# Eight PSUM banks dealt anew: four for the scores, one in two halves for the attention's outputs

## The chip, the cores and the metric

The kernel runs on one core of one Trainium2 chip. The metric is the device time of one execution in microseconds (us); before the change it is 2353.01 us, the median of three runs (2352.11 to 2354.78).

## What is computed

One inference step of a transformer layer with two kinds of attention side by side. For 2048 new frames of one stream and for 16 new frames of each of 8 running streams (with 512 cached frames each):

```
h  = rms_norm(x) * (1 + scale) + shift          # modulation from c @ w_ada
qa, ka, va, za, qb, kb, vb, zb, ga, gb = split(h @ w_in)
oa = (softmax(q1 k1) - lam * softmax(q2 k2)) @ va    # 4 heads, width 2 x 64, rotated q and k
ob = a @ vb                                          # 8 heads, width 64, where, with z = q.k / 8:
     a[q,k] = sigmoid(z[q,k]) * product over j > k of sigmoid(-z[q,j])      # "stick breaking"
ya = (rms_norm(oa) * silu(za)) @ w_branch_a;  yb = (ob * silu(zb)) @ w_branch_b
x  = x + gate * ((sigmoid(ga) * ya + sigmoid(gb) * yb) @ w_out)
y  = rms_norm(x)
```

Both masks are causal (by chunks of 64 for the first kind). The outputs are y and the new keys and values.

## The kernel before

Matrix operands are held as pairs of 16-bit numbers, a high and a low part, so a product takes up to three matmuls. Work goes by tiles of 128 rows: 16 tiles of the new stream, and tile number 16 (NT) for the 8 x 16 running frames.

**First stage** (some 145 us). `modulation` multiplies the conditioning by w_ada; `modulated` (L1052) scales and turns x by matmuls with a diagonal (L1065) into h, which is stored in HBM as hT_d.

**Attention.** Eight units follow one another: unit u is head u // 2 of the softmax kind (kind 0, even u) or a pair of stick-breaking heads (kind 1, odd u). Each unit goes through 17 tiles. For each tile `project` multiplies h by the unit's weights: 24 matmuls into a bank "mm" (L427), and in six of the eight units as much again for a gate, into bank "t" (L494). ACT, DVE and POOL turn the result into q, k and v. `transpose_qk` turns q and k through bank "t" (L507, L511; evacuated in L521, L522). `scores` makes the scores of one tile against all keys up to it, in chunks of up to 512 keys: two matmuls into a bank "s" (L629, L630), and a mask on the diagonal chunk (L633). A softmax chunk is read by DVE with a running maximum (L548). A stick-breaking chunk is read by ACT, which puts sigmoid(z) into SBUF and sigmoid(-z) back into the bank (both by the helper at L119), and then by a DVE scan along the keys (L606), which makes the products; POOL multiplies (L612). `turn` splits the weights into high and low parts (L562, L563, or L290, L295) and has SP's queue turn them by a transposing DMA into one of five tiles wt (L570). Two steps later `pv` multiplies them by v: three matmuls per block of 128 keys for kind 0 (L677 to L679), two for kind 1 (L681, L682), for both heads of the pair. The sum of one tile grows in a bank "o"; such a run of matmuls into one output is called a group. `natural` reads it out: ACT for kind 0 (L658), ACT and then DVE for kind 1 (L663, L664). There are 8 x 16 = 128 groups.

**Last stage** (from about 1805 us). For each tile, `inputs` and `transposed` (L1141, through bank "s") prepare the merged attention outputs, `branches` multiplies by the branch weights (L1289, bank "mm"), `output` by w_out in two halves of 512 columns (L1318, each half in a bank "o"). Beside it runs `sample`, the attention of the running streams over their caches (L745 to L753, banks "s"; L784, bank "t").

PSUM has eight banks of 128 x 512 numbers of 32 bits, and `BANKS` (L185) deals them out: 2 "mm", 3 "s", 1 "t", 2 "o". A tile of a tag takes the next free bank of that tag; where none is free, its first matmul waits for the readers of an earlier tile. In the first stage L1063 takes banks "s" and "o" in turn.

**What sets the order.** The program lists the pieces of a step (projection, scores, outputs) interleaved by estimated costs (`interleave`, L91; outputs between 0.1 and 1.0 of the step, V_LO and V_HI). From that list a scheduler makes the order of the instructions of each engine when the program is built: it goes through its own estimate of the time, and gives each engine the earliest listed instruction that is ready by it, a free bank included. On the chip each engine then runs its instructions in that fixed order, and waits by semaphores where the data or the bank isn't ready. All loads, stores and transposes are issued in order by SP: the h tiles (L404, three buffers hs), the transposes (L570), the stores of k, v and z (L475, L476, L478) and of outputs (L671).

Of the kernel before, what the change touches and what calls it, by code (L numbers as in the profile page):

```python
# [16 lines left out]
F32 = mybir.dt.float32  # L17
# [8 lines left out]
P = 128  # L26
# [83 lines left out]
def layer_kernel(ctx: ExitStack, tc: tile.TileContext, a: dict):  # L110
# [40 lines left out]
    def x_rows(t):  # L151
        return x_p[t * P : (t + 1) * P, :] if t < NT else x_s
# [17 lines left out]
    ps = ctx.enter_context(tc.tile_pool(name="ps", bufs=2, space=bass.MemoryType.PSUM))  # L170
# [11 lines left out]
    kvp = c01.enter_context(tc.tile_pool(name="kvp", bufs=2))  # L182
    stg = c01.enter_context(tc.tile_pool(name="stg", bufs=2))

    BANKS = {"mm": 2, "s": 3, "t": 1, "o": 2}  # L185

    def bank(tag, dt=F32):
        return ps.tile([P, 512 if dt == F32 else 1024], dt, tag=tag, name=f"ps_{tag}", bufs=BANKS[tag])

# [462 lines left out]
    def natural(U, t, po, pool=stg):  # L652

        kind = U["kind"]
        o = pool.tile([P, P], F32, tag="o", name="o")
        s = U["sc"][:, 5:6]
        if kind == 0:
            S.activation(out=o, in_=po[:, 0:P], func=AF.Identity, scale=s)  # L658
            return o
        ob = pool.tile([P, P], F32, tag="ob", name="ob", bufs=1)  # L660
        p4 = po[:, 0 : 2 * P].rearrange("p (c f d) -> p c f d", c=2, f=2)
        oh, ol = (x.rearrange("p (c d) -> p c d", c=2) for x in (ob, o))
        S.activation(out=oh, in_=p4[:, :, 1, :], func=AF.Identity, scale=s)  # L663
        V.scalar_tensor_tensor(out=ol, in0=p4[:, :, 0, :], scalar=s, in1=oh, op0=ALU.mult, op1=ALU.add)  # L664
        return o

    def store(U, t, o):
        ui = (U["h"] + 4 * U["kind"]) * P
        if U["kind"] == 0:
            sum_squares(o, P, osums[:, t, U["h"] : U["h"] + 1])  # L670
        load(out=o_d[t][:, ui : ui + P], in_=o)  # L671

    def pv_block(job, seg, po, wj, vt, first, last):

        wt, nb, c = seg["wt"], seg["hi"] - seg["lo"], job["c"]
        if job["U"]["kind"] == 0:
            T.matmul(po[:, 0:P], wt[:, wj, :], vt[:, :, 0, :], start=first, stop=False)  # L677
            T.matmul(po[:, 0:P], wt[:, wj, :], vt[:, :, 1, :], start=False, stop=False)
            T.matmul(po[:, 0:P], wt[:, nb + wj, :], vt[:, :, 0, :], start=False, stop=last)  # L679
        else:  # L680
            T.matmul(po[:, c * P : (c + 1) * P], wt[:, wj, :], vt[:, c, :, :], start=first, stop=False)  # L681
            T.matmul(po[:, c * P : c * P + 64], wt[:, nb + wj, :], vt[:, c, 0, :], start=False, stop=last)  # L682

    def pv(job):

        U, t, c = job["U"], job["t"], job["c"]
        segs = job["segs"] if U["kind"] == 0 else job["segs"][::-1]
        order = [(seg, j) for seg in segs for j in range(seg["hi"] - seg["lo"])]

        def block(i):  # L690
            seg, j = order[i]
            if i == 0 and (U["kind"] == 0 or c == 0):
                U["po", t] = bank("o")
            pv_block(job, seg, U["po", t], j, U["v"][seg["lo"] + j], i == 0, i == len(order) - 1)
            if i == len(order) - 1 and (U["kind"] == 0 or c == 1):
                store(U, t, natural(U, t, U.pop(("po", t))))

        return [(1.5, lambda i=i: block(i)) for i in range(len(order))]
# [194 lines left out]
    with tc.tile_pool(name="p0", bufs=1) as p0:  # L893
# [8 lines left out]
        def hp_tile(dt):  # L902
            hp = p0.tile([P, 4096], F32, tag="hp", name="hp", bufs=3)
            return hp.bitcast(dt) if dt != F32 else hp
# [23 lines left out]
        pt = bank("t")  # L928
# [33 lines left out]
        pt = bank("t")  # L962
# [89 lines left out]
        def modulated(g):  # L1052

            t0, w = GROUPS[g]
            nt = w // P
            box = {}

            def piece(k):
                if k == 0:
                    box["hp"] = hp = hp_tile(F16)[:, 0 : nt * 2 * D].rearrange("p (i a k n) -> p i a k n", a=2, k=KT, n=P)  # L1060
                    at_hand.update({t0 // P + i: hp[:, i, :, :, :] for i in range(nt)})
                hp = box["hp"]
                pt = bank("so"[k % 2])  # L1063
                for i in range(nt):
                    T.matmul(pt[:, i * P : (i + 1) * P], xs[g][i][:, k * P : (k + 1) * P], diags[g][:, i, :], start=True, stop=True)  # L1065
                tmp = p0.tile([P, 512], F32, tag="tmp", name="tmp", bufs=2)
                hi, lo = hp[:, :, 0, k, :], hp[:, :, 1, k, :]
                pv = pt[:, 0:w].rearrange("p (i n) -> p i n", n=P)
                tv = tmp[:, 0:w].rearrange("p (i n) -> p i n", n=P)
                if t0 < SEQ:  # L1070
                    S.activation(out=hi, in_=pv, func=AF.Identity, scale=ab[:, 0, k, 0:1], bias=ab[:, 1, k, 0:1])
                    V.tensor_scalar(out=tv, in0=pv, scalar1=ab[:, 0, k, 0:1], scalar2=ab[:, 1, k, 0:1],
                                    op0=ALU.mult, op1=ALU.add)
                else:
                    tb = tmp[:, 0:w].rearrange("p (b s) -> p b s", b=NB)
                    V.tensor_tensor(out=tb, in0=pt[:, 0:w].rearrange("p (b s) -> p b s", b=NB),
                                    in1=ab[:, 0, k, 1:9].unsqueeze(2).to_broadcast([P, NB, NS]), op=ALU.mult)
                    V.tensor_tensor(out=tb, in0=tb, in1=ab[:, 1, k, 1:9].unsqueeze(2).to_broadcast([P, NB, NS]), op=ALU.add)
                    S.copy(out=hi, in_=tv)
                G.tensor_tensor(out=lo, in0=tv, in1=hi, op=ALU.subtract)  # L1080
                if k == KT - 1:
                    load(out=hT_d[g], in_=hp)

            return [(1.0, lambda k=k: piece(k)) for k in range(KT)]

        def gates():
# [136 lines left out]
    for n in range(len(steps) + PV_LAG):  # L1223
        made, qk, vs = [], [], []
        if n < len(steps):
            u, t = steps[n]
# [28 lines left out]
    with ExitStack() as c2:  # L1255
# [16 lines left out]
        def gate_rows(i, n):  # L1272

            pg = bank("t")
            gsm = s2.tile([P, 512], F32, tag="sg", name="gsm", bufs=2)
            load(out=gsm[0:9, :], in_=gate_d[:, n * 512 : (n + 1) * 512])
            T.matmul(pg, sel[0:9, i * P : (i + 1) * P], gsm[0:9, :], start=True, stop=True)
            return pg
# [27 lines left out]
        def output(t, st, box):  # L1306

            def half(j):
                if j == 0:
                    box["x"] = s2.tile([P, D], F32, tag="x", name="x2", bufs=2)  # L1310
                    load(out=box["x"], in_=x_rows(t))
                x = box["x"]
                c = slice(j * 512, (j + 1) * 512)
                po = bank("o")
                n = 0
                for yi, wi in ((0, 0), (0, 1), (1, 0)):
                    for k in range(KT):
                        T.matmul(po, st["y"][:, yi * 8 + k, :], wo[j * 4 + k // 2][:, wi, k % 2, :], start=(n == 0), stop=(n == 3 * KT - 1))  # L1318
                        n += 1
                m = s2.tile([P, 512], F32, tag="sg", name="m", bufs=2)  # L1320
                if t < NT:
                    V.scalar_tensor_tensor(out=m, in0=po, scalar=st["f"][:, 1:2], in1=gate[:, c], op0=ALU.mult, op1=ALU.mult)
                else:
                    S.activation(out=m, in_=po, func=AF.Identity, scale=st["f"][:, 1:2])
                    V.tensor_tensor(out=m, in0=m, in1=gate_rows(1, j), op=ALU.mult)
                G.tensor_tensor(out=x[:, c], in0=m, in1=x[:, c], op=ALU.add)
            return [(5.2, lambda j=j: half(j)) for j in range(2)]
# [73 lines left out]
```

## Time and profile before

| | |
|---|---|
| median of three runs | 2353.01 us |
| the profiled execution | 2352.26 us |
| its span, first to last instruction | 2350.5 us |
| PE (matmul) busy | 2124.5 us, 90% |
| DVE (vector) busy | 1729.8 us, 74% |
| ACT (scalar) busy | 1635.9 us, 70% |
| POOL busy | 687.0 us, 29% |
| DMA | 453.74 MB, mean 193 GB/s |
| TensorE clock granted, mean | 0.965 of full speed |

Lines named Lnnn are lines of the kernel before. PE is the matmul engine, PEld its weight loads, SP the queue that issues DMAs. A row of waits reads "who waits, the tile and line it waits to write <- whom it waits for: us in total, times, longest us". A row of groups reads "line, engine, operation, out<-in, shapes, count | busy us, mean ns of one | idle us of the engine before it <- what ended that idle time". A row of the timeline reads "start us, length us, engine, line, operation, tiles, shapes, count". Matmuls overlap in the records: one of 512 columns is shown with 380 ns, but a new one starts about every 0.22 us.

### The profile page before, as it was taken

The numbers are of one execution on the slowest core, as the hardware profiler recorded it, in microseconds if no ns is written. First come the engines' busy times: TensorE is split into PE (matmuls) and PEld (weight loads), VectorE is DVE, ScalarE is ACT, GpSimd is POOL, SyncE is SP. The second block draws the span as 40 slices with busy tenths as digits, with TensorE's granted clock in tenths as the row PEclk, the third lists the DMA queues.
The fourth block names the chain that finished last, engine by engine and source line by source line (L and its number), as shares of the span: only waits on it lengthen the run. The fifth ranks groups of instructions, "written<-read, shape, count | busy, mean of one in ns | idle before, by whom it ended". The sixth has DMA issues, their size and how long they took to land. (4 is left out here: it accounts for less than half of the span.)

```text
span 2350.5 us, 42534 instructions
## 1 busy us (share of the span) xinstructions
PE 2124.5 (90%) x15272; PEld 1147.0 (49%) x15272; DVE 1729.8 (74%) x3604; ACT 1635.9 (70%) x3148; POOL 687.0 (29%) x563
## 2 busy tenths in 40 slices
PE   5898898998999899899999989999995789889998
PEld 3554454444555444445554544555553344445453
DVE  4847865779775567988666798867678777878763
ACT  4557777777786777778677787866677666666541
POOL 1533012345310233632023364203334222222221
PEclk8999999999999999999999999999997899999999
DMA  9766669887795898878678796866677999998621
GB/s 336 254 203 175 158 137 252 196 195 158 188 238 134 192 222 195 174 171 197 137 178 204 170 196 171 203 150 162 151 170 166 290 254 255 282 238 239 178 100 55
DMA packets 843572, 453.74 MB, mean 193 GB/s; under 512 B 538234, under 2 KB 786346, under 8 KB 842848
## 3 DMA queue, kind: packets, MB, share of 16 engines
q1 hardware_dynamic: 842412, 450.63, 77.2%
q8 instruction: 119, 1.95, 0.3%
q14 instruction: 93, 0.76, 0.1%
q10 hardware_dynamic: 948, 0.39, 0.1%
HBM read 249.80 MB, written 73.44 MB: 138 GB/s over the span
## 5 line engine op out<-in xcount | busy, mean ns | idle before, releaser
L612 POOL TENSOR_TENSOR sc_p<-sc_p,sc_n 128x127 f32<-128x127 f32 (+7 forms) x192 | 311.3, 1625 | 885.5 <-DVE sc_n L606 870.5
L427 PE MATMUL ps_mm<-wb,hs 128*128 128x512 f16 x1632 | 413.4, 380 | 5.0 <-DMA hs<-hT_d 3.2
L427 PEld LDWEIGHTS <-hs 128*128 128x128 f16 x3120 | 273.8, 99 | 252.3 <-issue 12.5
L427 PE MATMUL ps_mm<-wa,hs 128*128 128x512 f16 x1488 | 378.4, 385 | 3.4 <-DVE v L295 2.4
L606 DVE TENSOR_TENSOR_SCAN sc_n<-ps_s,sc_n,zero_t 128x512 f32<-128x512 f32 x192 | 245.3, 1278 | 75.6 <-ACT ps_s L119 72.5
L629 PE MATMUL ps_s<-k,qst 128*128 128x512 f16 (+3 forms) x640 | 225.7, 354 | 47.2 <-DVE sc_n L606 33.7
L563 DVE TENSOR_TENSOR sc_n<-sc_p,sc_n 128x128 f16<-128x128 f32 (+7 forms) x192 | 219.9, 1150 | 51.3 <-ACT sc_n L562 50.8
L494 PEld LDWEIGHTS <-hs 128*128 128x128 f16 x1632 | 154.8, 98 | 182.9 <-DVE qst L522 7.8
L119 ACT ACTIVATE sc_p<-ps_s,usc 128x512 f32<-128x512 f32 (+3 forms) x320 | 203.7, 636 | 44.9 <-PE ps_s L630 34.7
L630 PE MATMUL ps_s<-k,qst 128*128 128x512 f16 (+3 forms) x640 | 225.6, 354 | 0.0
L681 PE MATMUL ps_o<-v,wt 128*128 128x128 f16 x1088 | 175.3, 226 | 36.3 <-DMA wt<-sc_n 36.2
L562 ACT CAST sc_n<-sc_p 128x128 f16<-128x128 f32 (+7 forms) x192 | 154.5, 808 | 65.7 <-POOL sc_p L612 65.0
L494 PE MATMUL ps_t<-wb,hs 128*128 128x512 f16 x816 | 193.5, 381 | 7.0 <-DVE qst L522 6.9
L119 ACT ACTIVATE ps_s<-ps_s,usc 128x512 f32<-128x512 f32 (+3 forms) x328 | 198.6, 606 | 0.0
L494 PE MATMUL ps_t<-wa,hs 128*128 128x512 f16 x816 | 192.1, 380 | 1.7 <-ACT qst L522 1.7
L1318 PE MATMUL ps_o<-wo,wb 128*128 128x512 f16 x816 | 188.6, 386 | 0.7 <-ACT wb L1142 0.7
L682 PE MATMUL ps_o<-v,wt 128*128 128x64 f16 x1088 | 160.1, 198 | 0.0
L681 PEld LDWEIGHTS <-wt 128*128 128x128 f16 x1088 | 106.3, 102 | 104.6 <-DMA wt<-sc_n 48.2
L606 DVE TENSOR_TENSOR_SCAN sc_n<-ps_s,zero_t 128x128 f32<-128x128 f32 (+3 forms) x128 | 104.3, 815 | 48.4 <-ACT ps_s L119 46.3
L548 DVE TENSOR_SCALAR_CACHE_REDUCE sc_p<-ps_s,usc 128x512 f32<-128x512 f32 (+3 forms) x160 | 106.1, 664 | 42.3 <-PE ps_s L630 27.2
L682 PEld LDWEIGHTS <-wt 128*128 128x128 f16 x1088 | 103.9, 101 | 56.3 <-issue 1.9
L548 DVE TENSOR_SCALAR_CACHE_REDUCE sc_n<-ps_s,usc 128x512 f32<-128x512 f32 (+3 forms) x160 | 106.2, 664 | 31.5 <-PE ps_s L630 13.7
(345 smaller groups left out, 4478.0 us busy)
## 6 DMA issues: line engine op xcount, KB each, us to landing
hs<-hT_d SPq DMA_DIRECT2D x130, 512.0 KB, 4.5
g_d<-gt SPq DMA_DIRECT2D x68, 256.0 KB, 4.2
wb<-g_d SPq DMA_DIRECT2D x26, 512.0 KB, 5.7
out_dram<-pr SPq DMA_DIRECT2D x204, 64.0 KB, 2.1
z_d<-pr SPq DMA_DIRECT2D x136, 64.0 KB, 1.8
o_d<-o SPq DMA_DIRECT2D x136, 64.0 KB, 2.4
hs<-z_d SPq DMA_DIRECT2D x17, 512.0 KB, 5.0
hs<-o_d SPq DMA_DIRECT2D x17, 512.0 KB, 6.4
```

What stands on the lines that cost most here:

```text
L119: i = S.activation(**kw)
L427: T.matmul(box["p"], box["h"][:, hi, k, :], U["w"][k][:, wi, :], start=(n == 0), stop=(n == 3 * KT - 1))
L494: T.matmul(box["g"][:, 0:gw], box["h"][:, hi, k, :], U["wg"][k // per][:, k % per, wi, :], start=(j == 0), stop=(j == 3 * KT - 1))
L548: V.tensor_scalar(out=dst[:, lo : lo + n], in0=p[:, 0:n], scalar1=sc_pos, scalar2=None, op0=ALU.mult, op1=ALU.max, accum_out=job["mx"][:, ...
L563: V.tensor_tensor(out=lo, in0=src, in1=hi, op=ALU.subtract)
L606: V.tensor_tensor_scan(out=dst[:, lo : lo + n][:, ::-1], data0=src[:, 0:n][:, ::-1], data1=zero_t[:, 0:1].to_broadcast([P, n]), initial=fi ...
L612: G.tensor_tensor(out=p[:, 0:m], in0=p[:, 0:m], in1=n[:, 1 : m + 1], op=ALU.mult)
L629: T.matmul(p[:, 0:n], qst[:, c, :], kk[:, c, 0:n], start=True, stop=False)
L630: T.matmul(p[:, 0:n], qst[:, 2 + c, :], kk[:, c, 0:n], start=False, stop=not diag)
L681: T.matmul(po[:, c * P : (c + 1) * P], wt[:, wj, :], vt[:, c, :, :], start=first, stop=False)
L682: T.matmul(po[:, c * P : c * P + 64], wt[:, nb + wj, :], vt[:, c, 0, :], start=False, stop=last)
L1318: T.matmul(po, st["y"][:, yi * 8 + k, :], wo[j * 4 + k // 2][:, wi, k % 2, :], start=(n == 0), stop=(n == 3 * KT - 1))
```

## The change

The banks are dealt anew: four for "s", none for "o", and one tile `outputs_of` that is allocated once and takes the eighth bank. The attention's outputs use its columns 0 to 255 and 256 to 511 in turn, one group after the other. A softmax group uses 128 of its 256 columns, a stick-breaking group all 256. The first stage's turns use "s" alone. In the last stage the first half of an output tile uses the whole of `outputs_of`, the second a bank "s". In what follows, line numbers are those of the kernel before.

```diff
-    BANKS = {"mm": 2, "s": 3, "t": 1, "o": 2}
+    BANKS = {"mm": 2, "s": 4, "t": 1}
+
+    outputs_of = ps.tile([P, 512], F32, tag="o", name="ps_o", bufs=1)
+    out_at = [0]
...
             if i == 0 and (U["kind"] == 0 or c == 0):
-                U["po", t] = bank("o")
+                out_at[0] ^= 1
+                U["po", t] = outputs_of[:, out_at[0] * 256 : out_at[0] * 256 + 256]
...
-                pt = bank("so"[k % 2])
+                pt = bank("s")
...
-                po = bank("o")
+                po = bank("s") if j else outputs_of
```

No instruction is added or removed: matmuls, evacuations and DMAs are the same in number and shape. The scheduler makes its order anew.

## The prediction

> **What bounds the kernel now.** I read the page's span first, then the busy time of each engine by stage (windows cut where the attention's score matmuls begin, near 145 us, and where the attention's last scores have run, near 1805 us), then PE's waits inside the attention, then the chain that ended last.
>
> ```profile
> span 2350.5 us, 42534 instructions
> ```
>
> ```profile
> 0.00:145.00 145.00, 112.51 (x761) 72.58 (x762) 85.68 (x239) 69.72 (x132) 59.03 (x73) 0.91 0.79 266
> 145.00:1805.00 1660.00, 1536.84 (x10773) 830.51 (x10770) 1251.51 (x2545) 1249.27 (x2572) 510.99 (x411) 0.98 0.77 181
> 1805.00:2350.00 545.00, 475.20 (x3740) 243.88 (x3740) 392.63 (x821) 316.93 (x446) 116.98 (x81) 0.94 0.79 210
> ```
>
> The columns after the length are PE, PEld, DVE, ACT and POOL busy time, then PE's granted clock, the DMA share and GB/s. In the attention PE works 1536.8 of 1660 us; DVE and ACT reach 75% each. So PE is the engine to follow, and what can be won without taking matmuls away is its 123 us of idle time. What ended that idle time:
>
> ```profile
> PE ps_s L629 <- DVE sc_n L606: 33.7, 41, 2.3
> PE ps_o L681 <- DMA wt<-sc_n: 25.9, 24, 2.4
> PE ps_o L677 <- DMA wt<-sc_n: 18.4, 13, 3.1
> PE ps_s L629 <- DVE sc_p L548: 9.4, 8, 3.8
> PE ps_t L507 <- DVE k L295: 7.8, 9, 1.7
> PE ps_t L494 <- DVE qst L522: 6.9, 4, 3.3
> PE ps_t L507 <- ACT gt L497: 4.5, 6, 1.1
> PE ps_mm L427 <- DVE v L295: 4.2, 2, 2.4
> PE ps_mm L427 <- DMA hs<-hT_d: 4.0, 4, 1.6
> PE ps_s L629 <- DVE sc_n L548: 3.7, 3, 2.3
> PE ps_t L494 <- ACT qst L522: 1.7, 1, 1.7
> ```
>
> Each row has the sum, the number of times and the longest, in us. The eleven make 120.2, nearly all of the 123. Three kinds matter. **Score banks** (L629 waits for the reader of a bank to let it go): 33.7 + 9.4 + 3.7 = 46.8. **Turned weights** (L681, L677 wait for a transposing DMA): 25.9 + 18.4 = 44.3. **The projection's side** (the other six): 29.1. No row shows PE waiting for an output bank.
>
> PE's queue is in order, so such a stall delays all that is behind it. From 2208 us to 2340 the chain that ended last is nearly all matmuls, as in this piece:
>
> ```profile
> 2295.17 8.85 PE ps_o L1318 x41
> 2304.02 0.89 PE ps_s L1141 x16
> ```
>
> So what PE saves in the attention is not covered by a slower engine at the end.
>
> **The change, part by part.** It adds and removes no matmul, no evacuation and no DMA. It changes which bank is written, and the scheduler, which knows the banks, then gives another order to the same instructions. I compare both orders as built, counting matmuls, and turn counts into time with this row of the timeline:
>
> ```profile
> 481.10 5.34 PE L494 MATMUL ps_t<-wa,hs 128*128 128x512 f16 x24
> ```
>
> 24 matmuls of 512 columns in 5.34 us: 0.22 us each. The narrow matmuls of the outputs take less, so times from counts are upper estimates.
>
> *1. A fourth bank for the scores.* A bank of a stick-breaking chunk is held through two sigmoids and a scan:
>
> ```profile
> L606 DVE TENSOR_TENSOR_SCAN sc_n<-ps_s,sc_n,zero_t 128x512 f32<-128x512 f32 x192 | 245.3, 1278 | 75.6 <-ACT ps_s L119 72.5
> ...
> L119 ACT ACTIVATE sc_p<-ps_s,usc 128x512 f32<-128x512 f32 x224 | 157.2, 702 | 38.7 <-PE ps_s L630 34.7 <-PE ps_s L633 3.8
> ...
> L119 ACT ACTIVATE ps_s<-ps_s,usc 128x512 f32<-128x512 f32 x224 | 151.6, 677 | 0.0
> ```
>
> 0.70 + 0.68 + 1.28 = 2.66 us at least, beyond the matmuls. In the built order, between the last matmul in such a bank and the first of its next tenant stand 50 other matmuls at the median before, 67 after (37 and 48 for the softmax heads); 247 of the score matmuls carry a wait for the scan before, 161 after. 17 more matmuls are about 3.7 us of lead, against a mean wait of 33.7 / 41 = 0.8 us and a longest of 2.3. Bounds: 46.8 gained, or 0, if ACT and DVE fall back as far as the scores run ahead. I take 28, a little over the drop in the count, for lead is long against the waits.
>
> *2. Turned weights.* With scores earlier, a stick-breaking segment has 195 matmuls between its last score and the first use of its turned weights, 162 before. But weights that wait longer hold one of five wt buffers longer, and SP, whose queue is also in order, already stands for them:
>
> ```profile
> SPq L404 <- PE ps_t L494: 61.8, 25, 8.1
> SPq L570 <- PE ps_o L682: 51.6, 30, 4.0
> ```
>
> 145 of the transposes wait for PE to free a buffer in the built order before, 180 after. Behind each waiting transpose stand the stores of keys, values and outputs, the weight loads and the next h tile (L404). Bounds: 44.3 gained; or a loss of 51.6 x 35 / 145 = 12.5, if SP's extra standing came through to PE whole. I take a gain of 10.
>
> *3. One bank for the outputs.* Halves in turn look like two buffers. Who reads an output:
>
> ```profile
> L658 ACT ACTIVATE o<-ps_o,usc x64: 345/365/382, 163.7 to 1601.1; 128x128 f32<-128x128 f32 x64
> L663 ACT ACTIVATE ob<-ps_o,usc x64: 343/372/459, 341.0 to 1820.4; 128x128 f32<-128x128 f32 x64
> L664 DVE SCALAR_TENSOR_TENSOR o<-ps_o,usc,ob x64: 319/330/351, 342.0 to 1820.8; 128x128 f32<-128x128 f32 x64
> ```
>
> As built, the first output matmul of a group waits for the readers of the group just before it in 104 of 128 groups (16 before): a half gives no second buffer. Behind that wait stands all of PE. What two banks hide today, from the timeline:
>
> ```profile
> 987.81 0.19 PE L682 MATMUL ps_o<-v,wt 128*128 128x64 f16 x1
> ...
> 988.08 0.39 ACT L663 ACTIVATE ob<-ps_o,usc 128x128 f32<-128x128 f32 x1
> ...
> 988.27 0.22 PE L681 MATMUL ps_o<-v,wt 128*128 128x128 f16 x1
> ```
>
> ```profile
> 992.45 0.32 DVE L664 SCALAR_TENSOR_TENSOR o<-ps_o,usc,ob 128x128 f32<-128x128 f32 x1
> ```
>
> The old group ends at 988.00, the next starts at 988.27, and the old bank is free only at 992.77, 4.8 us after its last matmul: with one bank PE would stand 4.5 us here. The scheduler now puts other matmuls there: between the last of a stick-breaking group and the next group's first stand 10 at the median before, 35 after (about 7.7 us); fewer than 15 in 39 cases before, 4 after. Softmax groups: 43 and 41, fewer than 15 in 15 and 1. Bounds: 0, and 64 x 0.365 + 64 x (0.372 + 0.330) = 68.3 if nothing stood between and each reader came at once. I take 6: five uncovered groups at a little over 1 us each, near the cover.
>
> **By bank or by address.** No row of before shows PE writing one half of a bank while another engine reads the other. Were halves independent, term 3 would be 0; as built it is by bank. The Trainium skill, "PSUM — Partial Sum Buffer", section "PSUM bank collisions raise a hardware error", has engines kept apart by bank and quadrant of partitions, whatever the columns: a rule against this change, with which the built order agrees and which no run here shows yet. By it the sum below is -13; by halves it would be (20 + 6) x 2/3, that is -17 and 2335.
>
> *4. The projection's side.* To run scores sooner and outputs later, something loses slack. An h buffer that PE frees is read again after 122 matmuls at the median before, 108 after; fewer than 40 (8.8 us) in none of 125 before, in 5 of 117 after. Its load needs this to land, after SP has come to it:
>
> ```profile
> hs<-hT_d SPq DMA_DIRECT2D x130, 512.0 KB, 4.5
> ```
>
> I add a third to the 29.1, 9 us; bounds 0 and 29, a doubling.
>
> *5. Before and after the attention.* The first stage alternated over five banks and now has four. Four wait rows of L1065 there sum to 8.5, the first and the last:
>
> ```profile
> PE ps_o L1065 <- DVE tmp L1072: 3.5, 3, 2.4
> ...
> PE ps_s L1065 <- DVE tmp L1072: 1.4, 2, 0.8
> ```
>
> I add 3, bounds 0 and 8.5. In the last stage five banks serve the same uses (the sample's scores, turned operands, two output halves); output halves may now wait behind samples, and turned operands find a fourth bank:
>
> ```profile
> PE ps_s L753 <- DVE dsc L548: 5.1, 1, 5.1
> ```
>
> I take 0, bounds -5.1 and +5.1: this one stall, the longest of a score bank there, gone or doubled.
>
> **The sum.** -28 - 10 + 6 + 9 + 3 + 0 = -20. What is late next: a score that starts sooner meets its evacuation and its k and q tiles sooner, and part of each stall comes back at the next of the eleven rows. I choose to keep two thirds: -13. The profiled execution took 2352.3 us (span 2350.5), 0.7 below the median of 2353.0. 2352.3 - 13 = **2339 us**.
>
> **The rivals.**
> - *Outputs become PE's wait* (slower). If ACT and DVE come to L663 and L664 later on the chip than the scheduler thought, as in the 4.8 us above, PE stands at the first output matmul of a group. It decides where that standing passes the 26 us that the other terms win, 0.2 us for each of 128 groups. At the full 68.3, all of it kept: 2352 - 26 + 68 = 2394; with half the groups uncovered: 2352 - 26 + 34 = 2360. For it: the readers' 4.8 us, and DVE and ACT three quarters busy. Against: 35 matmuls of cover. Chance 0.2.
> - *SP's queue becomes the bound* (slower). More transposes stand for a wt buffer, and the next h tile stands behind them. With the bad ends of terms 2 and 4: -28 + 12.5 + 6 + 29 + 3 = +22.5, two thirds of it +15: 2367. For it: the 145 to 180, and SP's two rows, 113 us of standing today. Against: of that standing only 4.0 us reach PE's row for hs. Chance 0.1.
> - *The waits only move.* DVE and ACT set the pace within each burst, the fourth bank fills, and PE stands as long under other rows: 2352, within 5. For it: eleven rows of small stalls, none dominant. Against: 75% busy engines leave room to catch up. Chance 0.08.
> - *A denser PE gets a lower clock.* The three stages show 0.91, 0.98 and 0.94. One hundredth less over the attention costs 1537 x 0.01 / 0.98 = 15.7 us: 2339 + 16 = 2355. For it: nothing but the spread. Against: the densest stage has the highest clock. Chance 0.05.
> - *Nearly all of the score waits go and the weights' waits halve*: -47 - 22 + 18 = -51, two thirds or all of it kept: 2318 to 2301. Against: the wt buffers. Chance 0.07.
>
> **How the numbers follow.** Forecast 0.5 (2318 to 2347: two thirds of -51, and two thirds of -7, term 1 at 15), outputs 0.2 (2357 to 2394), SP 0.1 (about 2367), moved waits 0.08, clock 0.05, large gain 0.07. 0.2% of the time, 4.7 us, is about what a measurement of this kernel tells from no change. Faster 0.5 + 0.07 = 0.57, same 0.08 + 0.05 = 0.13, slower 0.3. The range 2318 to 2368 leaves out the large gain (0.07) and the outputs rival's upper part (0.12). The forecast's own range is 2318 to 2347.
>
> **What would show it.** Term 1: the row L629 waiting for L606 in the attention falls from 33.7 to some 13, and the three L629 rows from 46.8 to 19. Term 2: L681 and L677 for wt sum to about 34. Term 3: new rows, L681 waiting for DVE o L664 and L677 for ACT o L658, of some 6 together. Term 4: L427 for hs and L507 for k rise by some 9. PE's busy time in the attention stays near 1537. It is wrong if the new rows of term 3 pass 26, if L427 for hs passes 20, or if the L629 rows keep their 46.8.

## The result and the profile after

The changed kernel takes 2361.23 us (median of eight, 2356.89 to 2365.94), the kernel before 2353.05 beside it: a ratio of 1.0032, with a 95% interval of 1.0018 to 1.0047. It is slower by some 8 us; the forecast was 14 us faster. The time lies inside the range, on the side that had a chance of 0.3.

The page of the changed kernel gives its span, in a profiled execution of 2365.94 us, the longest of the eight:

```profile
span 2364.2 us, 42534 instructions
```

The windows of the same kernel, cut as in the prediction:

```profile
145.00:1805.00 1660.00, 1534.38 (x10721) 831.89 (x10720) 1247.56 (x2540) 1243.88 (x2568) 511.00 (x411) 0.97 0.78 181
1805.00:2364.00 559.00, 488.26 (x3801) 251.34 (x3798) 398.04 (x827) 320.85 (x451) 121.66 (x82) 0.92 0.79 206
```

In the attention PE stands idle for 125.6 of the 1660 us, against 123.2 before (1660 less PE's busy time, here and in the prediction's row): nothing was won. The timeline has the last score chunk of the attention 3.2 us later, first before, then after:

```profile
1800.77 0.38 PE L629 MATMUL ps_s<-k,qst 128*128 128x512 f16 x1 [0.52 <-DVE sc_n L606]
```

```profile
1803.99 0.59 PE L632 MATMUL ps_s<-k,qst 128*128 128x512 f16 x1 [0.38 <-DVE sc_n L609]
```

The rest of the two executions' difference isn't standing behind the attention. In these 1660 us 52 fewer matmuls run than before (10721 against 10773), and behind them 61 more (3801 against 3740): there PE is busy for 13.1 us longer, and idle for 70.7 us against 69.8. So the changed kernel leaves the attention with more work undone, later by more than the 3.2 us. That fewer matmuls fill nearly the same busy time, at a granted clock of 0.97 against 0.98, says that part of the loss is speed and not standing.

PE's waits in the attention of the changed kernel (line numbers are three or four higher than before: L632 is L629, L510 is L507, L497 is L494, L500 is L497, L430 is L427, L680 and L684 are L677 and L681, L667 is L664):

```profile
PE ps_s L632 <- DVE sc_n L609: 20.7, 16, 2.8
PE ps_o L680 <- DMA wt<-sc_n: 18.7, 12, 3.8
PE ps_mm L430 <- DMA hs<-hT_d: 17.3, 13, 3.0
PE ps_t L510 <- ACT gt L500: 14.8, 6, 3.4
PE ps_t L510 <- DVE sc_n L608: 9.5, 3, 3.2
PE ps_t L497 <- DVE qst L525: 9.5, 4, 2.5
PE ps_t L497 <- ACT qst L525: 7.1, 1, 7.1
PE ps_t L510 <- DVE k L298: 5.0, 3, 1.7
PE ps_s L632 <- DVE sc_n L551: 4.9, 5, 2.0
PE ps_o L684 <- DMA wt<-sc_n: 4.5, 5, 1.3
PE ps_s L632 <- DVE qst L525: 4.3, 2, 2.2
PE ps_s L632 <- DVE sc_p L551: 3.2, 3, 2.1
...
PE ps_o L684 <- DVE o L667: 0.5, 2, 0.3
```

By kind: score banks 46.8 to 28.8 (three L632 rows; the fourth, for qst, is a score that waits for its turned q), turned weights 44.3 to 23.2, readers of outputs 0 to 0.5 (and one stall of 5.8 us behind the attention). That is 39 us less. The rows that write bank t went from 20.9 to 46.8 (with 0.9 in two small rows). Not all of that is the bank: L510's wait for k (7.8 before, 5.0 after) is a turn that waits for its own input. The row for hs went from 4.0 to 17.3, the new one for q took 4.3: with the other rows of bank mm (4.2 before, 4.3 after), the projection's side took 44 more. What was taken from some rows came back in others. Whether one part of the change gains and the other loses, the rows of this kernel alone can't say.

### The profile page after: what moved, and what is told of

The parts are those of the page before. It is cut to its first block, busy times and chain, and to the rows that moved or that the text cites. A ratio compares the mean times of both kernels' runs of the same rounds, so it can differ in the third digit from the quotient of the medians.

```text
span 2364.2 us, 42534 instructions
## 1 busy us (share of the span) xinstructions
PE 2132.5 (90%) x15272; PEld 1153.1 (49%) x15272; DVE 1732.3 (73%) x3604; ACT 1634.4 (69%) x3148; POOL 690.7 (29%) x563
## 5 line engine op out<-in xcount | busy, mean ns | idle before, releaser
L430 PEld LDWEIGHTS <-hs 128*128 128x128 f16 x3120 | 285.7, 99 | 308.2 <-DMA hs<-hT_d 22.7
L430 PE MATMUL ps_mm<-wb,hs 128*128 128x512 f16 x1632 | 402.0, 383 | 13.3 <-DMA hs<-hT_d 10.5
L430 PE MATMUL ps_mm<-wa,hs 128*128 128x512 f16 x1488 | 365.2, 382 | 8.3 <-DMA hs<-hT_d 6.8
L632 PE MATMUL ps_s<-k,qst 128*128 128x512 f16 (+3 forms) x640 | 225.1, 354 | 33.1 <-DVE sc_n L609 20.7
L566 DVE TENSOR_TENSOR sc_n<-sc_p,sc_n 128x128 f16<-128x128 f32 (+7 forms) x192 | 228.7, 1198 | 33.6 <-ACT sc_n L565 33.3
L497 PEld LDWEIGHTS <-hs 128*128 128x128 f16 x1632 | 156.4, 99 | 194.0 <-issue 10.5
L497 PE MATMUL ps_t<-wb,hs 128*128 128x512 f16 x816 | 196.9, 386 | 7.0 <-DVE qst L525 7.0
L497 PE MATMUL ps_t<-wa,hs 128*128 128x512 f16 x816 | 193.5, 385 | 9.6 <-ACT qst L525 7.1
L684 PE MATMUL ps_o<-v,wt 128*128 128x128 f16 x1088 | 152.5, 227 | 15.8 <-DMA wt<-sc_n 9.3
L685 PE MATMUL ps_o<-v,wt 128*128 128x64 f16 x1088 | 142.3, 199 | 0.0
L684 PEld LDWEIGHTS <-wt 128*128 128x128 f16 x1088 | 106.1, 103 | 55.5 <-DMA wt<-sc_n 16.9
L551 DVE TENSOR_SCALAR_CACHE_REDUCE sc_p<-ps_s,usc 128x512 f32<-128x512 f32 (+3 forms) x160 | 106.4, 665 | 31.8 <-PE ps_s L633 24.1
L1322 PEld LDWEIGHTS <-wb 128*128 128x128 f16 x816 | 79.2, 99 | 101.4 <-issue 7.4
```

The lines of the kernel that those rows point to most:

```text
L430: T.matmul(box["p"], box["h"][:, hi, k, :], U["w"][k][:, wi, :], start=(n == 0), stop=(n == 3 * KT - 1))
L497: T.matmul(box["g"][:, 0:gw], box["h"][:, hi, k, :], U["wg"][k // per][:, k % per, wi, :], start=(j == 0), stop=(j == 3 * KT - 1))
L551: V.tensor_scalar(out=dst[:, lo : lo + n], in0=p[:, 0:n], scalar1=sc_pos, scalar2=None, op0=ALU.mult, op1=ALU.max, accum_out=job["mx"][:, ...
L566: V.tensor_tensor(out=lo, in0=src, in1=hi, op=ALU.subtract)
L632: T.matmul(p[:, 0:n], qst[:, c, :], kk[:, c, 0:n], start=True, stop=False)
```

## The experiments

All times are medians; each ratio is to the kernel before, measured beside it, with its 95% interval. "Held" means that TensorE's instructions keep, by order alone and without a wait, the order that the scheduler made for the kernel named. A kernel held in its own order is built the same on every engine, so the holding itself changes nothing. The other engines' orders remain the scheduler's, so what is called the order below is TensorE's, with what the scheduler puts around it on the other engines.

| run | banks mm, s, t, outputs, other | TensorE's order | us | ratio |
|---|---|---|---|---|
| before | 2, 3, 1, 2 | own | 2353.05 | 1 |
| after | 2, 4, 1, 1 halved | own | 2361.23 | 1.0032 [1.0018, 1.0047] |
| out_alone | 2, 3, 1, 1 halved, 1 idle | own | 2342.11 | 0.9956 [0.9938, 0.9973] |
| out_and_scores | 2, 3 + 1, 1, 1 halved | own | 2363.14 | 1.0039 [1.0026, 1.0052] |
| out_and_mm | 3, 3, 1, 1 halved | own | 2363.22 | 1.0041 [1.0025, 1.0056] |
| out_and_t | 2, 3, 2, 1 halved | own | 2336.36 | 0.9926 [0.9912, 0.9941] |
| t_order_free | 2, 3, 1 + 1, 1 halved | own | 2325.49 | 0.9875 [0.9861, 0.9888] |
| banks_only | 2, 3 + 1, 1, 1 halved | held as out_alone | 2345.93 | 0.9974 [0.9960, 0.9988] |
| mm_bank_only | 2 + 1, 3, 1, 1 halved | held as out_alone | 2346.00 | 0.9963 [0.9950, 0.9976] |
| t_bank_only | 2, 3, 1 + 1, 1 halved | held as out_alone | 2346.14 | 0.9962 [0.9949, 0.9974] |
| order_only | 2, 3, 1, 1 halved, 1 idle | held as out_and_scores | 2395.34 | 1.0194 [1.0176, 1.0212] |
| before_in_out_order | 2, 3, 1, 2 | held as out_alone | 2341.22 | 0.9957 [0.9940, 0.9973] |
| out_in_before_order | 2, 3, 1, 1 halved, 1 idle | held as before | 2422.38 | 1.0298 [1.0276, 1.0319] |

Two statements on record are wrong. The section on the kernel gives the gate to six of the eight units; it is the four stick-breaking ones. And where the expectations below speak of matmuls "at the median" between output groups (6 and 30) or between uses of an h buffer (57, 129, 76), these are lower quartiles; the medians are 23 and 37, and 95, 174 and 108.

### The two parts of the change, one at a time

*out_alone* takes the single output bank and leaves the freed bank out of the attention; first and last stage still deal five banks:

```diff
-    BANKS = {"mm": 2, "s": 3, "t": 1, "o": 2}
+    BANKS = {"mm": 2, "s": 3, "t": 1, "x": 1}
...
-                pt = bank("so"[k % 2])
+                pt = bank("s") if k % 2 == 0 else outputs_of if k % 4 == 1 else bank("x")
...
-                po = bank("o")
+                po = bank("x") if j else outputs_of
```

with `outputs_of` and its halves as in the change. *out_and_scores* then gives the bank to the scores (`p = bank("x" if turn_at[0] % 4 == 0 else "s")`, with a count of the chunks). *out_and_t* gives it to t (`"t": 2` in place of `"x": 1`).

> The outputs' single bank in halves is the only edit in the attention; scores keep three banks, and the eighth bank serves only the first and last stage, which deal their banks as before. If the single output bank is what costs (rival), this is slower than before by 8 us or more (2361 and up), with rows of output matmuls waiting for L658 or L664 of 10 us and more. If the loss comes from the scores running ahead (theory), this is within 5 us of before (2348 to 2358), the score waits stay near 47 us, and the waits on bank t and on the h tiles stay near 29.

> As out_alone, and every fourth score chunk of the attention takes the eighth bank; first and last stage deal as before. Theory (scores ahead push the gate's and projection's evacuations back in ACT's queue): as slow as the changed kernel, 2357 to 2366, the score waits fall below 32 us, the waits on bank t and on h tiles rise to 50 and more, and there are 20 or more PE stalls over 2 us in the attention (12 before). Rival (the last stage's new deal costs): back at 2348 to 2356, since the last stage is as before.

> Outputs in one bank; the freed bank goes to t (gate and transposes), scores keep three. Theory: the t waits (L494, L507; 21 us before, 47 after) nearly vanish, and this is faster than before: 2330 to 2347. Rival (the single output bank costs): slower than before, 2357 and up. Rival (waits only move): within 5 us of before.

The single output bank alone gains 0.4%, which neither expectation had (2348 to 2358, or 2361 and up). The fourth score bank takes 0.8% back. With out_and_scores as slow as the changed kernel though its last stage is dealt as in out_alone, the last stage's dealing isn't the cause. At bank t the same freed bank is no loss: the rows in which PE waited there for a reader (L507 for gt, L494 for qst, 13.1 us before) are gone, and the 19 us that remain are turns that wait for k and q, their own inputs. PE's waits up to the last score, of out_alone:

```profile
PE ps_o L684 <- DMA wt<-sc_n: 19.1, 17, 2.6
PE ps_s L632 <- DVE sc_n L609: 18.8, 18, 3.0
PE ps_mm L430 <- DMA hs<-hT_d: 17.8, 9, 7.0
PE ps_o L680 <- DMA wt<-sc_n: 13.4, 13, 2.1
PE ps_o L684 <- DVE o L667: 8.0, 3, 4.0
...
PE ps_s L632 <- DVE sc_p L551: 5.0, 4, 3.9
PE ps_s L632 <- DVE sc_n L551: 3.8, 4, 2.1
```

The score rows are at 27.6 with three banks, where the expectation had some 47, and the turned weights at 32.5: most of what the prediction gave to the fourth score bank has already come with the single output bank. Of out_and_scores, its score rows:

```profile
PE ps_s L633 <- DVE sc_n L609: 18.1, 14, 3.2
...
PE ps_s L633 <- DVE sc_p L551: 7.0, 3, 4.6
...
PE ps_x L633 <- DVE sc_n L609: 4.5, 3, 2.0
```

They sum to 29.6, no less than with three banks.

*before_later_outputs* moves the scheduler's list by a little (V_LO from 0.1 to 0.12 in the kernel before), to see what another order does by chance.

> A control on the kernel before: the outputs of a step begin at 0.12 of it, not at 0.1; banks as before. It changes no count and hardly any cover, only the order that the scheduler makes. If the order's luck alone is worth as much as the change (rival), this differs from before by 5 us or more; if not, it is within 3 us (2350 to 2356).

It took 2352.39 us, 0.9995 [0.9982, 1.0008]: no difference. The order of out_alone wasn't pushed in this way, so that its 0.4% isn't chance rests on this one control.

### Why bank t waits: two theories that fell

*four_scores_shared* and *three_scores_shared* let projection, turns and gates draw on one pool (`BANKS = {"p": 3, "s": 4}`, and `{"p": 4, "s": 3}`, with `{"mm": "p", "t": "p"}`).

> The changed kernel, but the two banks of the projection and the one of the turns and gates become one pool of three that both take from (four score banks and the halved output bank stay). Theory T, the single bank t: with four score banks the scores move ahead and the users of bank t come to stand close behind one another (6 of 65 gates follow a turn by fewer than 8 matmuls, 1 before), so a late reader of that bank stops PE; the rows of PE waiting to write ps_t in the attention sum to some 47 us in the changed kernel, 21 before. With the pool no gate follows a turn in the same bank by fewer than 28 matmuls, so T expects these rows to fall below 15 us and the time to 2335 to 2345 (2361 less two thirds of 30 to 40). Rival S, running the scores ahead costs by itself (h tiles, turned weights, SP's queue, longer stalls wherever they fall): within 6 us of the changed kernel, 2355 to 2367, with the stalls under other rows.

> As the run before in this list, but with three score banks and a pool of four for projection, turns and gates. Theory T (bank t is what the fourth score bank hurt): three or four score banks differ little once the pool is there, this one within 6 us of its neighbour, both at 2333 to 2345. Rival S (the scores' running ahead costs by itself): this one 2330 to 2338, as with the freed bank given to t (2336.4), and at least 15 us faster than the one with four score banks.

They took 2408.32 us (1.0232 [1.0211, 1.0252]) and 2439.94 us (1.0368 [1.0344, 1.0392]), far from both theories, and the one with four score banks is the faster. Two rows of four_scores_shared up to its last score show where the time went (L299 and L458 belong to the projection's readers):

```profile
PE ps_t L511 <- DVE k L299: 20.2, 12, 6.9
PE ps_t L515 <- DVE qbuf L458: 14.0, 5, 4.9
```

A pool is dealt in turn, so a turn can now stand behind the slow readers of a projection. But k and qbuf are also a turn's own inputs, and the rows don't tell the two apart. The two runs show the price of such a pool, and nothing on either theory.

*after_norms_late* lists each sum of squares (L272) two steps behind its load:

```diff
+            held.append((st, dst, scale))
...
+            if i >= LAG:
+                st, dst, scale = held.pop(0)
+                sum_squares(st, 1024, dst, scale=scale)
+                free.append(st)
```

> The changed kernel, but each sum of squares of a cache or weight tile (L272) is listed two steps after its load, so that ACT doesn't come to it before the load has landed. Theory A: the long stalls at bank t begin with ACT standing for such a load (4.1 us from 403.98 us on, with PE standing 3.4 us at bank t behind the gate's evacuation); six of the stalls at t over 2 us have it at their root. A expects ACT's idle time for these loads, 44 to 48 us, to fall below 15, the ps_t rows to fall from 47 to some 25 and the time to 2340 to 2350. Rival, that another evacuation in ACT's or DVE's queue is as late in its place: the loads' standing goes, PE's stalls at t stay over 40 us, the time stays within 5 us of 2361.

2359.37 us, 1.0029 [1.0017, 1.0041]: theory A falls as far as this goes. ACT's idle time for these loads fell only from 48.5 to 33.1 us, so the test is a weak one, but bank t's rows moved by 4 us.

*out_and_mm* gives the freed bank to the projection (`"mm": 3`).

> The halved output bank with three score banks, and the freed bank given to the projection (three for it, one for t). Theory T: bank t is single, but the scores run no further ahead than before, so it is as the halved output bank alone: 2338 to 2346. Rival S: the same for its own reason. Rival H, the h tiles: with a third projection bank the h buffers turn over sooner (57 matmuls at the median between free and next use, 129 with the bank at t, 76 in the changed kernel), so the row of PE waiting for hs passes 25 us and the time is 2345 to 2360. The run tells whether any freed bank helps, or only one at t.

```profile
PE ps_mm L430 <- DMA hs<-hT_d: 32.8, 22, 4.2
```

Rival H comes closest: 2363.22 us and 32.8 us for the h tiles, a little over the time it gave. T and S fall here: both had 2338 to 2346. So the same bank loses as much with the projection as with the scores, under another row. That took the question off bank t: what do these two orders have in common?

### Order or bank

The recorder that holds the order (`order` is the other kernel's, as a list of matmuls):

```diff
-    V, S, G, T = nc.vector, nc.scalar, nc.gpsimd, nc.tensor
+    V, S, G, T = nc.vector, nc.scalar, nc.gpsimd, Recorded(nc.tensor)
...
+        for before, after in zip(order, order[1:]):
+            tc.add_manual_dep(self.made[after].ins, self.made[before].ins.name, NOSYNC, reason="order of another program")
```

*banks_only* is out_and_scores with the order of out_alone, *order_only* is out_alone with the order of out_and_scores.

> The halved output bank alone gained 11 us (2342), and a fourth bank for the scores on top of it lost 21 (2363). The two kernels differ in the bank that every fourth score chunk takes and in the order that the scheduler makes of it. Here the scores have the fourth bank, but TensorE's instructions are held, by order alone and without a wait, in the order of the kernel with three score banks. Theory O, order: what costs is that the scheduler, seeing a bank free, moves scores ahead of other matmuls; the bank itself only takes waits away. O expects 2330 to 2343 here, with the score rows (28 us with three banks) below 15 and the rows of bank t near the 13 of that order. Rival B, the bank: with more chunks in flight ACT and DVE come later to everything else, whatever PE's order: 2355 or more here.

> The mirror of the run before: three score banks, but TensorE's instructions in the order that the scheduler made for four. Theory O expects the loss to be all here: 2363 or more, up to 2390, since the same order now also waits for a bank that isn't there, with the rows of bank t near the 35 us of that order and the score rows over 33. Rival B expects 2342 to 2352.

In a held kernel all matmuls stand at L91 and all turns at L95, and the other lines shift: in these two, L644 is the scan L606, L586 is L548, L535 is L497, L333 is L295, L703 is L664. PE's waits up to the last score, of banks_only:

```profile
PE ps_o L91 <- DMA wt<-sc_n: 38.0, 29, 3.2
PE ps_mm L91 <- DMA hs<-hT_d: 18.5, 9, 7.5
PE ps_t L95 <- DVE k L333: 11.6, 7, 2.4
PE ps_s L91 <- DVE sc_p L586: 8.4, 4, 7.4
PE ps_t L95 <- ACT gt L535: 6.1, 3, 3.3
PE ps_o L91 <- DVE o L703: 5.1, 5, 3.3
PE ps_s L91 <- DVE sc_n L644: 4.5, 3, 2.5
```

and of order_only:

```profile
PE ps_s L91 <- DVE sc_n L644: 55.0, 56, 2.5
PE ps_mm L91 <- DMA hs<-hT_d: 21.3, 12, 4.2
PE ps_o L91 <- DMA wt<-sc_n: 21.0, 16, 3.7
PE ps_s L91 <- DVE sc_p L586: 18.6, 20, 4.1
```

The bank by itself does what a bank should: at the held order the score rows fall from 27.6 to some 15 (with three small rows). But the turned weights rise from 32.5 to 38.0 and bank t, with its small rows, from 13 to 24, and the ratio, 0.9974, is no better than out_alone's 0.9956. PE comes sooner to the next thing that isn't ready. Theory O had asked for 2330 to 2343 and got 2346, so its "the bank only takes waits away" was too hopeful. Its other half holds: the order made for four banks costs 0.65% where it has four (0.9974 to 1.0039), and 2.4% where it has three (0.9956 to 1.0194). Rival B, by which the fourth bank costs at any order, falls. In order_only O had the kind of wait wrong: the rows of bank t sum to 14 us and not to 35, and the score rows alone to 80.

The built orders show what the scheduler did with the bank. Between the last score matmul in a bank and the first of the tile that comes next into it stand 43 others at the median in the kernel before and in out_alone, 58 in out_and_scores, 61 in banks_only. But fewer than 15 (some 3.3 us at 0.22 us each, against the 2.66 us of a chunk's readers) stand there in 14, 17, 22 and 12 of some 637 cases. With its own order the fourth bank didn't make the short cases fewer; at the held order it did. That the scheduler puts scores earlier until the bank is, by its own estimate, just free again is argued from these counts. And counts alone don't tell the waits: with 43 and 14 the kernel before has 46.8 us in its score rows, with 43 and 17 out_alone has 27.6.

*before_in_out_order* and *out_in_before_order* ask the same of the output bank.

> The banks of the kernel before (two for the outputs, three for the scores), with TensorE's instructions in the order that the scheduler made for the single halved output bank. Theory O for the gain of that bank: an output bank that is missing can gain nothing by itself, so the 11 us come from the order it forces (30 matmuls at the median between output groups instead of 6). O expects the gain here as well, and the 8 us of waits for readers of outputs gone: 2332 to 2344. Rival: the gain lies in the other engines' orders or is chance: 2350 to 2356.

> The single halved output bank, with TensorE's instructions in the order of the kernel before (6 matmuls at the median between output groups). This is the price that the prediction's first rival put on the bank, 68 us if nothing stands between a group and its readers. Theory O expects the waits at the first matmul of an output group for its readers to be 50 to 150 us and the time 2390 to 2480. Rival, that the halves do act as two buffers on the chip or that the readers come early enough: 2350 to 2365.

PE's waits for readers of outputs in out_in_before_order (L702 is L664, L696 is L658):

```profile
PE ps_o L91 <- DVE o L702: 107.4, 36, 8.6
...
PE ps_o L91 <- ACT o L696: 6.3, 10, 1.5
```

With one bank for the outputs and the old order, PE waits 114 us for readers and the kernel is 3% slower, 72 us: the prediction's first rival, priced at 68, at the place where it would have been right. With two banks and the new order the gain is the same as with one (0.9957 and 0.9956). So the single bank by itself gains nothing: at the order made for it it costs nothing, at the old one 3%. What gains the 0.4% is the order that it forces on the scheduler, with output groups spread out instead of following one another.

By the Trainium skill, "PSUM — Partial Sum Buffer", section "PSUM bank collisions raise a hardware error", engines are to be kept apart by bank and quadrant, not by address. The 107.4 us agree that this kernel is kept apart so, halves or not; no run here shows halves without such a wait.

### The other places for the freed bank, with the order held

*t_bank_only* and *mm_bank_only* hold out_alone's order and let the attention's turns and gates, or its projection, take the freed bank in turn with their own (first and last stage as in out_alone). *t_order_free* is t_bank_only with the scheduler's own order. *t_later* is out_and_t with V_LO 0.12.

> The halved output bank with the freed bank given to the turns and gates of the attention in turn with bank t, but TensorE held in the order of the halved output bank alone, which was made for one bank t. Theory O (a bank at a held order only moves the waits): the ps_t rows fall from 13 to below 6 us, other rows take most of it, the time is 2336 to 2346. Rival (bank t itself is what limits): as with the scheduler's own order for two such banks, 2330 to 2338.

> The same banks as in the run before, but the scheduler makes its own order for them (first and last stage dealt as with the halved output bank alone). Theory O: the order carries the gain, 2332 to 2340, and at least 4 us faster than the run before. Rival: the same time as the run before, within 3 us.

> The halved output bank with the freed bank given to the projection as a third one in the attention, but TensorE held in the order made for two. Theory O: the 21 us that this bank lost with the scheduler's own order were the order's (projection moved ahead of the h tiles' loads), so 2338 to 2346 here, with the row of PE waiting for hs at some 18 us as in the held order, not 33. Rival, that the third bank itself draws the h tiles and costs: 2352 or more.

> The freed bank given to t (2336), with the outputs listed from 0.12 of a step on instead of 0.1: the same small push that moved the kernel before by nothing (0.9995). If the gain belongs to the dealing of the banks, 2331 to 2342. If it hangs on one chance order, 2345 or more.

At the held order the three places give 0.9974, 0.9963 and 0.9962: none differs from the idle bank's 0.9956 by more than the intervals. With an order made for it, the bank gives 1.0039 with the scores, 1.0041 with the projection, 0.9875 with t. t_later took 2332.55 us (0.9906 [0.9892, 0.9919]), so the gain at t isn't one chance order. t_order_free, at 2325.49, is the fastest of all, below the 2332 to 2340 that theory O gave. It differs from out_and_t in the first and last stage, where t has one bank and not two; from the last score on it takes 560 us, out_and_t 568.

What the good order does: in the stick-breaking units an h tile is let go when the gate's matmuls have read it (L494), and SP, which loads the next h tile, stands for them. SP's waits up to the last score, of t_bank_only (L446 is L404, L91 the gate in bank t or x):

```profile
SPq L446 <- PE ps_x L91: 37.4, 11, 9.0
SPq L446 <- PE ps_t L91: 34.7, 13, 8.9
```

and of t_order_free (L411 is L404, L501 is L494):

```profile
SPq L411 <- PE ps_x L501: 10.3, 5, 3.8
SPq L411 <- PE ps_t L501: 9.8, 4, 4.1
```

72 us became 20, and the row of PE waiting for hs, 17.8 in out_alone and 19.1 in t_bank_only, is gone from t_order_free's list. With a second bank to take in turn the gates could be put earlier: in the built orders the last matmul of a gate stands 43 others behind the projection's last at the median in t_order_free, 126 in out_alone. And h tiles came in time. The score rows, at 40.6, are higher than out_alone's 27.6, in the faster kernel:

```profile
PE ps_s L636 <- DVE sc_n L613: 34.5, 31, 3.1
...
PE ps_s L636 <- DVE sc_p L555: 4.9, 2, 2.9
...
PE ps_s L636 <- DVE sc_n L555: 1.2, 3, 0.5
```

That the gates' earlier place is the whole of the gain is argued from these rows and wasn't tried by itself. Its mirror, the order of t_order_free with a single bank t, wasn't tried: in that order six turns run while a gate is being summed, so one bank can't hold both.

## Why the prediction was wrong

- **Term 1, the fourth bank for the scores (-28 of 46.8): the step that failed.** The three rows fell by 18, and not through this bank: out_alone has them at 27.6 with three, the changed kernel at 28.8 with four. The prediction compared the built orders at their medians ("17 more matmuls are about 3.7 us of lead") and took the lead for slack. The scheduler had used it: the cases with fewer than 15 matmuls between went from 14 to 16. At a held order the bank takes 12 us from these rows and gives the time nothing; with its own order it costs 0.65% more. The size was misread as well: 28 was called "a little over the drop in the count", but from 247 to 161 is a drop of 35%, which is 16 of 46.8.
- **Term 2, turned weights (-10).** The rows fell by 21, but 11 of it, from 43.5 (up to the last score) to 32.5, is there without the fourth bank, through the output groups' new places: before_in_out_order, with two output banks, has 31.8.
- **Term 3, one bank for the outputs (+6).** The rows came to 0.5 in the attention and one stall of 5.8 behind it, so the cover was read rightly: 35 matmuls hide the readers. What was missed is the sign of the whole. The order that makes the cover is worth 0.4% by itself, and without that order the bank costs 3%. "By bank" was right: so it is built, and so PE waits.
- **Term 4, the projection's side (+9, bounds 0 and 29): far too small.** It rose by 44: bank t by 26, the row for hs by 13, the row for q by 4. The bounds doubled what stood there; they left out that PE, freed of other waits, comes to bank t before its readers do, which banks_only shows without any move of a matmul.
- **Term 5 (+3 and 0).** The attention's first score starts at 138.36 us against 138.31: the first stage cost nothing.
- **The sum.** -28 - 10 + 6 + 9 became, in the attention's rows, -18.0 - 21.1 + 0.5 + 43.6, that is +5; PE's idle time there went from 123.2 to 125.6. Keeping "two thirds" of a saving was no bound at all: here all came back. Nor does all that is won in the attention reach the end, as the prediction had it: out_alone has its last score 21 us sooner than before and its end 13, t_order_free 37 and 27. Why the last stage is longer there, no run shows.
- **The rivals.** Nearest was "the waits only move" (0.08), right for the bank by itself. The outputs' rival was wrong for this kernel and right for out_in_before_order. SP's rival is right in its rows and not in its effect: up to the last score SP stands 242 us for PE at its transposes, 160 before, and the row for hs grew; but all of SP's standing is 945 us against 946, and t_order_free, with 241 at the transposes, is the fastest.
- **The rival of a lower clock** (0.05, 15.7 us for one hundredth) can't be put aside. The profiled execution of the changed kernel shows 0.957 as a whole against 0.965, its eight 0.960 in the mean; 0.005 of 2361 us is 12 us, an estimate of the most that it can have cost, had PE been busy all that time. The cause isn't the rival's denser PE, for PE was no denser: the last section shows half clock behind windows in which PE stood for long. Nor does the clock alone tell the kernels apart: out_and_mm has 0.965 and takes 2363 us, out_alone 0.960 and 2342. How much of the 8 us it is was not tried.
- Of its signs, "L427 for hs passes 20" wasn't met (17.3), new output rows over 26 weren't either; bank t had none, and it was there that most of the time went.

What stays open: which single move in the order made for four score banks costs the 0.65%. Bank t's rows (35 against 13 in out_alone) are the largest difference, but the same rows come to 24 at the held order, where nothing is lost, and to 14 in order_only, which loses most. The place of the gates is a lead that wasn't tried: their last matmul stands 135 others behind the projection's in both orders that lose (out_and_scores, out_and_mm), 126 in out_alone, 110 before, 43 in t_order_free; the 110 before, in a slower kernel than out_alone, says that it isn't the only thing.

## What to carry to other kernels

Where a scheduler makes the order, a change of buffers is two changes: hold the old order and give the buffer, then let the order go, and time both; here each freed bank was worth nothing by itself, and between -0.8% and +0.9% through the order made for it (each against out_alone). Don't read cover from the median of the built order alone: here the median grew and the short cases stayed. Expect that a scheduler which takes the earliest ready instruction may spend a new buffer on running ahead. A freed buffer may do most at what lets a chain of others go (here the gate, which holds the h tile, which holds SP's queue), even if another row of waits is longer; one case shows it, in two orders.

## What the runs showed of the hardware that was not expected

The granted clock moves between full and half on a fixed grid of 3.41 us. In the changed kernel PE stands 3.14 us at a gate's reader:

```profile
507.83 0.27 PE L510 MATMUL ps_t<-id,k 128*128 128x128 f16 x2 [3.14 <-ACT gt L500]
```

The windows of that grid around it, and around a stall of 2.12 us that ends at 688.69:

```profile
504.85:508.27 3.42, 0.43 (x9) 0.43 (x9) 0.16 (x1) 2.21 (x4) 0.53 (x1) 1.00 1.13 219
508.27:511.68 3.41, 3.41 (x18) 1.64 (x15) 2.96 (x5) 3.26 (x7) 0.00 (x0) 0.50 0.92 146
685.76:689.17 3.41, 1.10 (x9) 0.63 (x8) 3.41 (x8) 3.41 (x10) 0.00 (x0) 1.00 0.26 55
689.17:692.58 3.41, 3.41 (x10) 1.22 (x9) 3.38 (x15) 3.03 (x8) 0.00 (x0) 0.50 1.07 195
```

and around a stall of 2.99 us that ends at 1216.58 and falls across two windows:

```profile
1211.42:1214.83 3.41, 2.17 (x28) 1.44 (x25) 2.36 (x4) 1.51 (x3) 2.01 (x1) 1.00 0.83 254
1214.83:1218.24 3.41, 1.66 (x8) 0.80 (x9) 1.40 (x4) 2.50 (x5) 0.00 (x0) 1.00 1.00 320
1218.24:1221.65 3.41, 3.41 (x18) 1.57 (x16) 0.83 (x3) 2.56 (x5) 0.00 (x0) 1.00 1.26 297
```

Where PE was busy for 0.43 or 1.10 us of a window, the next one runs at 0.50; where for 1.66 or 2.17, it stays at 1.00, though the stall is as long. From 145 to 1780 us of the changed kernel all 13 windows at full clock with PE busy under 40% are followed by one at half clock, 4 of 12 between 40% and 50%, and none of 430 above. In the traces of all eighteen kernels here it is 195 of 196, 55 of 152 and 4 of 7841. So the share of the window decides, and not the length of the stall. By the Trainium skill, "TensorE: Matmul & The Clock Gate", section "Part 1: The HAM clock gate (the "warmup" mystery)", the clock halves after an idle window of about 3.4 us and returns after a busy one; the trace agrees in the half and in the window, and differs in that a window need not be idle: a third of it busy was not enough.
